# A 512-token transformer stream on one core: modulation sums placed earlier in the first mixer, the softmax scale folded into the keys, the last square root taken on ScalarE

## The chip, the core and the metric

The kernel runs on one core of a Trainium2 chip. The metric is the device time in microseconds from the start to the end of one execution. The five engines of the core (TensorE, VectorE, ScalarE, GpSimd and SyncE) each run their own list of instructions strictly in order; they meet only at semaphores. In the rows below TensorE is PE, VectorE is DVE, ScalarE is ACT, GpSimd is POOL and SyncE is SP; SPq is the queue in which SP issues its transfers.

## What is computed

One stream of 512 tokens by 1024 features passes through two blocks. The first has a gated linear attention mixer and a convolutional feed-forward part, each closed by a residual with a modulation that depends on the conditioning vector `c`; the second has a retention layer and a layer of latent attention (MLA). Cut to what the change touches:

```python
def post_norm_residual(x, cs, w_mod, b_mod, ln_gain, ln_bias, sublayer):
    # shift, scale and gate come from cs @ w_mod + b_mod: the "modulation"
    ...

def gla_mixer(h, w_in, w_a2, b_a, norm_g, w_o):        # 4 heads, chunks of 64
    q, k, v, r, a_lr = jnp.split(h @ w_in, [...], axis=-1)
    log_a = jax.nn.log_sigmoid((a_lr @ w_a2 + b_a).astype(jnp.float32)) / GLA_TAU
    bcum = jnp.cumsum(chunks(log_a, GLA_DK), axis=3)
    q_dec = qf * jnp.exp(bcum)
    k_inv = kf * jnp.exp(-bcum)
    k_dec = kf * jnp.exp(blast - bcum)
    ...                                                # att, state, o
    o = o * lax.rsqrt(jnp.mean(o * o, -1, keepdims=True) + LN_EPS) * norm_g
    return (o * jax.nn.silu(r)) @ w_o

def mla_attention(q_nope, q_rope, k_nope, k_rope, v):  # 8 heads, blocks of 128 queries
    scale = (MLA_NOPE + MLA_ROPE) ** -0.5              # 192 ** -0.5
    sc = jnp.einsum('bqhd,bkhd->bhqk', qn_i, k_nope) + jnp.einsum('bqhr,bkr->bhqk', qr_i, k_rope)
    sc = sc.astype(jnp.float32) * scale
    sc = jnp.where(mask[None, None], sc, -jnp.inf)
    p = jax.nn.softmax(sc, axis=-1).astype(v.dtype)
    ...

def mla_layer(x, ...):
    y = (jax.nn.silu(gate) * o) @ w_out
    return x + rmsnorm(y, g_post)                      # the last root: rsqrt(mean(y*y) + eps)
```

## The kernel before

Every large product is done in three passes (`mm3`, L154, L155, L156): each factor is held as a high part, rounded to TensorE's fp32r format, and a low part with the rest, and the passes are high by high, high by low, low by high. `split` (L108) makes the two parts: ACT casts the high part (L114), DVE subtracts it for the low part (L115); with a scale, ACT scales while it rounds and DVE does multiply and subtract in one instruction (L118).

Weights come in 512 KB pieces: SP issues the transfer into `raw` (L127), ACT and DVE split the piece into `wsp`, TensorE multiplies. Both names are rings of four buffers. The ring of `raw` is shared: the pieces of the modulation matrices (`rawm`) take buffers from it as well, so a piece that waits for DVE holds a buffer that the next weights would need. There are two kinds of those pieces. Sixteen pieces of `l_mod` are each multiplied with a row and summed along it by one DVE instruction (L423; eight chunks, two sums each, into `mc1`), and thirty-two instructions over pieces of `mod_w` add up the gates (`macc`, L367).

The mixer runs in this order on TensorE: values of heads 0 and 1 with q and k, the low-rank decay input (`gla_a`, L597), the gate projection r for heads 0 and 1 with the decay products (L625) in between, then for heads 0 and 1 the inner products and state updates (`gla_inner`), then the same outputs (`gla_outer`, `po`), the values of heads 2 and 3 (`gla_v`), the transposes of the finished half u (`gate_T`, L462, evicted by DVE as `uT` through L118), inner products of heads 2 and 3, the gate r of those heads (`gla_r`, evicted by ACT as u at L485), and their outputs. The decay of a pair of heads goes through a chain on ACT and DVE: exponential and logarithm, a scan (L641), exponentials (L644, L648, L649), products with q and k (L662, L664), and splits into `qd` and `ki`, which the inner products (`aux<-qd,ki`) read.

Where the `l_mod` and `mod_w` pieces stand among this is set by the tuple `PLACE`: entry i says how many chunks are loaded and summed at the call `place(i)`. Within the constraints that `self.after(engine)` and priorities give, the framework orders the instructions of each engine when the program is built; on the chip nothing is reordered.

The MLA layer takes for each of 8 heads and 4 query blocks the scores in PSUM (`sc`), a maximum over the row (L1285, `mx`), that maximum times -scale (L1287, `nm`), the exponential with scale and bias (L1290, ACT), a reciprocal and a product for the weights `p`, and transposes of `p` (L1305). The final layer's `post_rms` (L1036) takes a reciprocal root per query block from `rsqrt` (L230): an integer guess and three Newton steps, nine DVE instructions on one value a row, and then scales and adds the residual (L1056 for blocks 0 to 2, L1081 in two halves for block 3, the last work of the program).

## Time and profile of the kernel before

| what | us |
|---|---|
| median of 3 runs (1264.45 to 1265.42) | 1265.42 |
| the profiled execution's own time | 1263.45 |
| its span, first to last instruction | 1261.7 |
| TensorE busy | 1223.8 (97%) |
| TensorE's wait for the first weights | 12.5 |
| VectorE busy | 816.8 (65%) |
| ScalarE busy | 540.4 (43%) |
| HBM traffic over the span | 117 GB/s |

A line of the timeline gives start, duration, engine, line of the kernel, operation, output and inputs, the number of like instructions joined in it, and in square brackets how long the engine had been idle before and whose work ended that. The durations of TensorE's matmuls overlap each other: the distance of two starts is what one costs.

### The profile page before, as it was taken

What the parts mean: (1) busy time and instruction counts of PE and PEld (TensorE: products, weight loads), DVE (VectorE), ACT (ScalarE), POOL (GpSimd) and SP (SyncE); (2) the same over time, 40 slices, a digit from 0 to 9 for tenths busy, and PEclk for the clock granted to TensorE, in tenths of its full rate; (3) what the DMA queues carried; (4) which work ended last, traced back from release to release, by engine and by line L of the source; (5) the groups of instructions that cost most, each with busy time, mean ns of one, the idle gap of its engine ahead of it and who ended that gap; (6) DMA issues with size and microseconds to landing.
All of it is one profiled execution on the core that took longest, in us unless ns stands there. A gap on an engine that the chain in (4) does not pass through costs nothing.

```text
span 1261.7 us, 16038 instructions
## 1 busy us (share of the span) xinstructions
PE 1223.8 (97%) x5982; PEld 1022.9 (81%) x5982; DVE 816.8 (65%) x1828; ACT 540.4 (43%) x958; POOL 3.6 (0%) x15
## 2 busy tenths in 40 slices
PE   6999899999999999999999999999999999999997
PEld 4777677898888888888788888888888888888886
DVE  6689587788442354445885648556454689677755
ACT  3585244443332133342443333433434347577631
POOL 0000000000000000000000000000000000000000
PEclk9999899999999999999999999999999999999999
DMA  9556275237222333334153232323332333212221
GB/s 363 201 168 231 79 254 172 64 120 231 87 98 100 101 91 93 100 123 128 63 157 90 85 89 85 92 84 92 117 105 96 109 98 107 70 51 75 84 84 68
DMA packets 133043, 148.44 MB, mean 118 GB/s; under 512 B 9825, under 2 KB 92152, under 8 KB 132964
## 3 DMA queue, kind: packets, MB, share of 16 engines
q1 hardware_dynamic: 132964, 147.40, 36.7%
q8 instruction: 47, 0.77, 0.3%
q14 instruction: 32, 0.26, 0.1%
HBM read 141.09 MB, written 6.29 MB: 117 GB/s over the span
## 4 chain that ended last, share of the span: by engine, by line
PE 84%; DVE 7%; ACT 4%; DMA 2%; issue 2%; SPq 0%; DVEq 0%; ACTq 0%
PE acc L154 25%; PE acc L156 25%; PE acc L155 25%; PE po L154 1%; PE po L156 1%; PE po L155 1%; DVE wsp L115 1%; DMA raw<-in_gla_w_in 1%; PE aux L154 1%; PE aux L155 1%; ACT wsp L114 1%; PE aux L156 1%; DVE rawm L423 1%; PE aux L931 1%; PE aux L1283 1%
## 5 line engine op out<-in xcount | busy, mean ns | idle before, releaser
L115 DVE TENSOR_TENSOR wsp<-raw,wsp 128x1024 fp32r<-128x1024 f32 (+1 forms) x162 | 195.5, 1209 | 183.8 <-ACT wsp L114 183.4
L114 ACT CAST wsp<-raw 128x1024 fp32r<-128x1024 f32 (+1 forms) x162 | 167.7, 1038 | 279.4 <-PE acc L156 239.3
L154 PE MATMUL acc<-hT,wsp 128*128 128x512 f32 (+1 forms) x640 | 244.0, 381 | 0.5 <-DVE v L115 0.5
L156 PE MATMUL acc<-hT,wsp 128*128 128x512 f32 (+1 forms) x640 | 243.0, 380 | 0.0
L155 PE MATMUL acc<-hT,wsp 128*128 128x512 f32 (+1 forms) x640 | 242.7, 379 | 0.0
L154 PE MATMUL acc<-wsp,hT 128*128 128x512 f32 (+2 forms) x448 | 170.2, 388 | 12.6 <-ACT wsp L114 12.5
L155 PE MATMUL acc<-wsp,hT 128*128 128x512 f32 (+2 forms) x448 | 171.6, 383 | 1.8 <-DVE wsp L115 1.8
L156 PE MATMUL acc<-wsp,hT 128*128 128x512 f32 (+2 forms) x448 | 170.1, 382 | 0.0
L154 PEld LDWEIGHTS acc<-hT,wsp 128*128 128x128 f32 x640 | 120.7, 189 | 23.6 <-DVE v L115 1.4
L155 PEld LDWEIGHTS acc<-hT,wsp 128*128 128x128 f32 x640 | 120.5, 188 | 22.0 <-issue 0.2
L156 PEld LDWEIGHTS acc<-hT,wsp 128*128 128x128 f32 x640 | 120.5, 188 | 21.9
L154 PEld LDWEIGHTS acc<-wsp,hT 128*128 128x128 f32 x448 | 85.0, 190 | 28.4 <-ACT wsp L114 13.0
L155 PEld LDWEIGHTS acc<-wsp,hT 128*128 128x128 f32 x448 | 84.7, 189 | 16.6 <-DVE wsp L115 2.5
L156 PEld LDWEIGHTS acc<-wsp,hT 128*128 128x128 f32 x448 | 84.5, 189 | 15.2
L154 PE MATMUL acc<-wsp,uT 128*128 128x512 f32 (+1 forms) x192 | 75.5, 393 | 0.0
L156 PE MATMUL acc<-wsp,uT 128*128 128x512 f32 (+1 forms) x192 | 74.9, 390 | 0.0
L155 PE MATMUL acc<-wsp,uT 128*128 128x512 f32 (+1 forms) x192 | 74.8, 389 | 0.0
L154 PE MATMUL acc<-wsp,p 128*128 128x512 f32 x144 | 56.8, 395 | 0.0
L155 PE MATMUL acc<-wsp,p 128*128 128x512 f32 x144 | 56.8, 395 | 0.0
L156 PE MATMUL acc<-wsp,p 128*128 128x512 f32 x144 | 56.8, 395 | 0.0
L833 DVE SCALAR_TENSOR_TENSOR cv<-acc,cols,cv 128x511 f32<-128x511 f32 x22 | 16.5, 749 | 58.1 <-ACT cv L832 58.1
L832 ACT ACTIVATE cv<-acc,cols 128x512 f32<-128x512 f32 x22 | 17.2, 780 | 83.1 <-PE acc L156 83.1
(358 smaller groups left out, 2063.6 us busy)
## 6 DMA issues: line engine op xcount, KB each, us to landing
raw<-in_w_in_a SPq DMA_DIRECT2D x48, 512.0 KB
raw<-in_ffn_w_up SPq DMA_DIRECT2D x44, 512.0 KB
raw<-in_ffn_w_down SPq DMA_DIRECT2D x22, 512.0 KB
ms<-in_l_mod SPq DMA_DIRECT2D x16, 512.0 KB
raw<-in_gla_w_in SPq DMA_DIRECT2D x16, 512.0 KB
rawm<-in_l_mod SPq DMA_DIRECT2D x16, 512.0 KB
rawm<-in_mod_w SPq DMA_DIRECT2D x16, 512.0 KB
raw<-in_w_out_a SPq DMA_DIRECT2D x16, 512.0 KB
```

Of the source, the lines that this page charges most:

```text
L114: nc.scalar.copy(hi, src)
L115: nc.vector.tensor_sub(lo, src, self.f(hi))
L154: mm(out, l[0], r[0], start=first, stop=False)
L155: mm(out, l[0], r[1], start=False, stop=False)
L156: mm(out, l[1], r[0], start=False, stop=last)
L423: nc.vector.scalar_tensor_tensor(m, m, 1.0, self.csr, op0=OP.mult, op1=OP.mult, accum_out=mc1[:, c, j:j + 1])
L832: nc.scalar.activation(t, p, AF.Identity, scale=cw[2 * NT + j], bias=cb[j])
L833: nc.vector.scalar_tensor_tensor(t[:, 1:], p[:, :T - 1], cw[NT + j], t[:, 1:], op0=OP.mult, op1=OP.add)
L931: nc.tensor.transpose(pu[:, b * P:(b + 1) * P], u[:, b, i * P:(i + 1) * P], self.ident)
L1283: nc.tensor.matmul(sc[:, :n], qrT[i][:, s], kr[i][:, :n], start=False, stop=i == 1)
```

## The change

It has three independent parts.

First, the places of the modulation sums. `PLACE` goes from seven entries to five: one chunk now stands before `gla_a`, two after the projection r as before, five chunks (ten sums) inside `gla_v`, at the last of its four weight pieces, and the two `mod_w` chunks after `gla_r` as before. The three chunks after the values' evictions and the three in heads 0 and 1 are gone from there. With it, all four weight pieces of r are split before the decay chain is written down, and the evictions of r to u are issued after that chain.

Second, in the MLA layer the factor 192 ** -0.5 is applied when the keys are split, so the scores come out scaled; the maximum is taken with a negation by the same instruction and the separate product is dropped.

Third, the reciprocal root of the final `post_rms` becomes a square root on ACT, a reciprocal and one Newton step.

```diff
--- before.py
+++ after.py
@@ -23,6 +23,7 @@
 ALPHA = 2.0 ** 0.25
 LN_EPS = 1e-5
 RMS_EPS = 1e-6
+SM = 192.0 ** -0.5
 FF = 2816
 MASKED = -float(2.0 ** 100)
 
@@ -245,6 +246,17 @@
             nc.vector.scalar_tensor_tensor(y, t, 1.5, y, op0=OP.add, op1=OP.mult)
         return y
 
+    def rsqrt_short(self, v):
+
+        nc = self.nc
+        y, t, h = self.small(1, "rs_y"), self.small(1, "rs_t"), self.small(1, "rs_h")
+        nc.scalar.activation(t, v, AF.Sqrt)
+        nc.vector.tensor_scalar_mul(h, v, -0.5)
+        nc.vector.reciprocal(y, t)
+        nc.vector.scalar_tensor_tensor(t, y, y, h, op0=OP.mult, op1=OP.mult)
+        nc.vector.scalar_tensor_tensor(y, t, 1.5, y, op0=OP.add, op1=OP.mult)
+        return y
+
     def transpose_split(self, dst, src, b, split_copy=True):
 
         nc = self.nc
@@ -271,7 +283,7 @@
     RAW, WSP, ST, MS = 4, 4, 6, 4
     GATES = {0: 4, 1: 5, 2: 6, 3: 7}
     WOUT = {6: (0, 2), 7: (2, 4)}
-    PLACE = (0, 2, 0, 0, 3, 3, 2)
+    PLACE = (1, 2, 0, 5, 2)
 
     def run(self):
         tc, nc = self.tc, self.nc
@@ -405,13 +417,6 @@
                 order = list(range(8)) + [(0, 2048), (0, 2560)]
 
                 def place(where):
-                    if where > 2:
-
-                        with self.after(nc.vector):
-                            return place_now(where)
-                    place_now(where)
-
-                def place_now(where):
                     for _ in range(self.PLACE[where]):
                         c = order.pop(0)
                         if isinstance(c, tuple):
@@ -424,19 +429,25 @@
                                                            accum_out=mc1[:, c, j:j + 1])
 
                 u = [out.tile([P, NB, 512], F32, name="u0")]
+                place(0)
                 arow = self.gla_a(ph, xT)
                 self.vectors(ph)
 
                 accs = [self.acc() for _ in range(NB)]
                 wi = a["gla_w_in"][0]
                 self.proj_t(xT, self.wsubs(wi, 2048, 2560, 0, 2), 512, None, accs=accs)
+                rest = [(k + 2, t) for k, t in self.wsubs(wi, 2048, 2560, 2, 8)]
                 with self.after(nc.tensor):
                     logs = self.gla_decay(ph, out, arow)
                 with tc.high_priority():
                     decay = [self.gla_sums(ph, out, logs, h) for h in range(2)]
-                place(0)
-                self.proj_t(xT, ((k + 2, t) for k, t in self.wsubs(wi, 2048, 2560, 2, 8)), 512,
-                            lambda b, ps: nc.scalar.activation(u[0][:, b, :], ps, AF.Silu), accs=accs)
+                chain = next(i for i in reversed(nc.cur_bb.bb.instructions) if i.engine == nc.scalar.engine)
+
+                def ev(b, ps):
+                    with tc.issue_after(chain):
+                        nc.scalar.activation(u[0][:, b, :], ps, AF.Silu)
+
+                self.proj_t(xT, rest, 512, ev, accs=accs)
                 place(1)
                 tril = out.tile([P, P], F32, name="tril")
                 nc.sync.dma_start(tril, a["k_tril"])
@@ -469,21 +480,23 @@
                     i0 = self.gla_inner(ph, p0, vh(0), tril)
                 with self.after(nc.scalar), self.after(nc.vector):
                     decay += [self.gla_sums(ph, out, logs, h) for h in range(2, 4)]
-                    place(3)
                 raw += self.gla_qk(xT, (2,))
                 i1 = self.gla_inner(ph, p1, vh(1), tril)
                 raw += self.gla_qk(xT, (3,))
-                place(4)
                 outer(0, i0)
                 outer(1, i1)
                 p2, p3 = prep(2), prep(3)
-                v = self.gla_v(out, xT, 1)
-                place(5)
+
+                def between():
+                    with self.after(nc.vector):
+                        place(3)
+
+                v = self.gla_v(out, xT, 1, between)
                 uT = [gate_T(0)]
                 i2 = self.gla_inner(ph, p2, vh(2), tril)
                 i3 = self.gla_inner(ph, p3, vh(3), tril)
                 self.gla_r(xT, 1, lambda b, ps: nc.scalar.activation(u[1][:, b, :], ps, AF.Silu))
-                place(6)
+                place(4)
                 for b in range(NB):
                     self.res[b] = self.main.tile([P, D], F32, tag=f"res{b}", name=f"res{b}")
                     nc.sync.dma_start(self.res[b], a["x"][0, b * P:(b + 1) * P, :])
@@ -565,10 +578,15 @@
         self.setup_late(ph)
         return xT, v, raws
 
-    def gla_v(self, out, xT, pr):
+    def gla_v(self, out, xT, pr, between):
+        def subs():
+            for k, t in self.wsubs(self.a["gla_w_in"][0], 1024 + pr * 512, 1536 + pr * 512):
+                if k == 6:
+                    between()
+                yield k, t
+
         v = out.tile([P, 2, NB, 512], F32R, tag="v", name="v")
-        self.proj_t(xT, self.wsubs(self.a["gla_w_in"][0], 1024 + pr * 512, 1536 + pr * 512), 512,
-                    lambda b, p: self.split(v[:, 0, b, :], v[:, 1, b, :], p))
+        self.proj_t(xT, subs(), 512, lambda b, p: self.split(v[:, 0, b, :], v[:, 1, b, :], p))
         return v
 
     def gla_r(self, xT, pr, evict):
@@ -1052,7 +1070,7 @@
             ms = self.small(1, "ms")
             nc.vector.tensor_add(ms, ss[b][:, 0:1], ss[b][:, 1:2])
             nc.vector.tensor_scalar(ms, ms, 1.0 / D, RMS_EPS, op0=OP.mult, op1=OP.add)
-            rs = self.rsqrt(ms)
+            rs = self.rsqrt_short(ms) if first else self.rsqrt(ms)
             nc.vector.scalar_tensor_tensor(self.res[b], y[b], rs, self.res[b], op0=OP.mult, op1=OP.add)
             done(b, slice(0, D))
 
@@ -1075,7 +1093,7 @@
                 nc.vector.tensor_scalar(sm, sm, 1.0 / D, RMS_EPS, op0=OP.mult, op1=OP.add)
             else:
                 nc.vector.tensor_scalar(ms, ms, 1.0 / D, sm, op0=OP.mult, op1=OP.add)
-                rs = self.rsqrt(ms)
+                rs = self.rsqrt_short(ms) if first else self.rsqrt(ms)
                 for s in (slice(0, 512), slice(512, D)):
                     r = self.res[b][:, s]
                     nc.vector.scalar_tensor_tensor(r, y[b][:, s], rs, r, op0=OP.mult, op1=OP.add)
@@ -1166,8 +1184,8 @@
                 ps = self.aux()
                 for b in range(NB):
                     nc.tensor.transpose(ps[:64, b * P:(b + 1) * P], krr[:, b, :], self.ident)
-                self.split(kr[0][0:64], kr[1][0:64], ps[0:64, :])
-                nc.scalar.copy(kr[0][64:128], ps[0:64, :])
+                self.split(kr[0][0:64], kr[1][0:64], ps[0:64, :], scale=SM)
+                nc.scalar.activation(kr[0][64:128], ps[0:64, :], AF.Copy, scale=SM)
                 for i, ts in ((0, qrT), (1, [kr])):
                     m = ph.tile([68, T], F32, name=f"mask{i}")
                     nc.sync.dma_start(m[64:68, :], a["k_msk"][i])
@@ -1260,9 +1278,10 @@
         nc.sync.dma_start(wl[:, 3:5, :], a["w_uk_2"][:, h * P:(h + 1) * P].rearrange("(k p) n -> p k n", p=P))
         ws = self.main.tile([P, 2, 5, P], F32R, tag="wsp", name="ws", bufs=self.WSP)
         self.split(ws[:, 0], ws[:, 1], wl)
-        for dst, src, k0, nk in ((qn, cqP, 0, 3), (kn, ckP, 3, 2)):
+
+        for dst, src, k0, nk, scale in ((qn, cqP, 0, 3, None), (kn, ckP, 3, 2, SM)):
             self.proj_f(src, [[(0, [(ws[:, 0, k0 + k, :], ws[:, 1, k0 + k, :]) for k in range(nk)])]],
-                        lambda n, p: self.split(dst[:, 0], dst[:, 1], p), nk=nk)
+                        lambda n, p: self.split(dst[:, 0], dst[:, 1], p, scale=scale), nk=nk)
         ps = self.aux()
         for b in range(NB):
             nc.tensor.transpose(ps[:64, b * P:(b + 1) * P], qr[:, b, h, :], self.ident)
@@ -1272,7 +1291,6 @@
 
     def mla_softmax(self, ph, qn, kn, kr, qrT):
         nc = self.nc
-        sm = 192.0 ** -0.5
         pr = []
         for b in range(NB):
             n = (b + 1) * P
@@ -1281,13 +1299,11 @@
             self.mm3(sc[:, :n], [qn[:, i, s] for i in range(2)], [kn[:, i, :n] for i in range(2)], True, False)
             for i in range(2):
                 nc.tensor.matmul(sc[:, :n], qrT[i][:, s], kr[i][:, :n], start=False, stop=i == 1)
-            mx = self.small(1, "mx")
-            nc.vector.reduce_max(mx, sc[:, :n], axis=AX.X)
             nm = self.small(1, "nm")
-            nc.vector.tensor_scalar_mul(nm, mx, -sm)
+            nc.vector.reduce_max(nm, sc[:, :n], axis=AX.X, negate=True)
             p = ph.tile([P, n], F32, tag=f"p{b}", name="p", bufs=2)
             den = self.small(1, "den")
-            nc.scalar.activation(p, sc[:, :n], AF.Exp, scale=sm, bias=nm, accum_out=den)
+            nc.scalar.activation(p, sc[:, :n], AF.Exp, bias=nm, accum_out=den)
             rd = self.small(1, "rd")
             nc.vector.reciprocal(rd, den)
             nc.vector.tensor_scalar_mul(p, p, rd)
```

On DVE, this is where before has the values' evictions (`v`) and the transposed u (`uT`) of the second half of the mixer:

```order
L722 SCALAR_TENSOR_TENSOR u_465<-po,rs_y,u_465 128x256 x4
L115 TENSOR_TENSOR v<-acc,v 128x512 x4
L423 SCALAR_TENSOR_TENSOR rawm,mc_462<-rawm,csr 128x1024 x4
L118 SCALAR_TENSOR_TENSOR uT_73<-aux,cols_494,uT_73 128x512
L423 SCALAR_TENSOR_TENSOR rawm,mc_462<-rawm,csr 128x1024 x2
L118 SCALAR_TENSOR_TENSOR uT_73<-aux,cols_494,uT_73 128x512 x3
L115 TENSOR_TENSOR kt<-aux,kt 128x384
```

Six sums thus stand between the last v and the last `uT`. And this is DVE of the change at the same evictions; `u_465` is u of heads 0 and 1, finished by L740:

```order
L740 SCALAR_TENSOR_TENSOR u_465<-po,rs_y,u_465 128x256 x4
L116 TENSOR_TENSOR v<-acc,v 128x512
L116 TENSOR_TENSOR wsp<-raw,wsp 128x1024
L116 TENSOR_TENSOR v<-acc,v 128x512 x2
L379 SCALAR_TENSOR_TENSOR macc<-rawm,cs,macc 128x512
L116 TENSOR_TENSOR v<-acc,v 128x512
L119 SCALAR_TENSOR_TENSOR uT_73<-aux,cols_500,uT_73 128x512 x4
L116 TENSOR_TENSOR wsp<-raw,wsp 128x1024
```

The six sums at L423 between `v` and `uT` are gone; the ten sums of `gla_v`'s call stand ahead of these lines, among the roots of the outputs of heads 0 and 1, and one sum for the gate (`macc`) now stands between the third and the fourth eviction of v.

On SP, before issues around the second values in this order (the `raw` at its top are the weights of `gla_v`, the four after the six `rawm` those of `gla_r`):

```order
L127 DMA raw<-in_gla_w_in 128x2x512 x3
L489 DMA res_1586<-in_x 128x1024
L127 DMA raw<-in_gla_w_in 128x2x512
L422 DMA rawm<-in_l_mod 128x1024 x6
L127 DMA raw<-in_gla_w_in 128x2x512 x4
L489 DMA res_1588<-in_x 128x1024
L364 DMA rawm<-in_mod_w 128x2x512 x2
```

The weights of `gla_r` come behind six pieces of `l_mod` there. The change has this order:

```order
L128 DMA raw<-in_gla_w_in 128x2x512 x4
L427 DMA rawm<-in_l_mod 128x1024
L502 DMA res_1586<-in_x 128x1024
L427 DMA rawm<-in_l_mod 128x1024 x9
L128 DMA raw<-in_gla_w_in 128x2x512 x4
L376 DMA rawm<-in_mod_w 128x2x512 x3
L502 DMA res_1588<-in_x 128x1024
```

The weights of `gla_r` still come behind all `rawm` of `l_mod`, but these now start right behind the weights of `gla_v`, and the first three pieces of `mod_w` follow the weights of `gla_r` directly.

In the first half, on DVE, before has behind the values of heads 0 and 1 the split of `was` (weights of the decay input), one weight piece, and `wr`, the low part of the weights of the decay products (made from `wf`):

```order
L115 TENSOR_TENSOR was<-wa,was 128x8x16
L115 TENSOR_TENSOR v<-acc,v 128x512 x4
L115 TENSOR_TENSOR wsp<-raw,wsp 128x1024
L618 TENSOR_TENSOR wr<-wf,wr 32x512
L348 COPY cols_494<-aux 128x127
L348 COPY cols_508<-aux 128x24
L601 TENSOR_TENSOR a_488<-acc,a_488 32x512
```

There `wr` comes behind one weight piece. The change:

```order
L428 SCALAR_TENSOR_TENSOR rawm,mc_462<-rawm,csr 128x1024
L116 TENSOR_TENSOR v<-acc,v 128x512 x4
L428 SCALAR_TENSOR_TENSOR rawm,mc_462<-rawm,csr 128x1024
L116 TENSOR_TENSOR was<-wa,was 128x8x16
L360 COPY cols_500<-aux 128x127
L360 COPY cols_514<-aux 128x24
L116 TENSOR_TENSOR wsp<-raw,wsp 128x1024
L619 TENSOR_TENSOR a_494<-acc,a_494 32x512
L116 TENSOR_TENSOR wsp<-raw,wsp 128x1024 x3
L636 TENSOR_TENSOR wr<-wf,wr 32x512
```

Two sums of the first chunk now stand around the evictions of v, and `wr` comes behind three more weight pieces. On TensorE the four decay products (`aux<-a,wr`) go from behind 24 products of r to behind 38.

## Rows read from the trace of the kernel before

**Rows 1.** Windows: us, busy us of PE, PEld, DVE, ACT, POOL, clock, DMA, GB/s

```profile
122.00:147.90 25.90, 25.70 (x128) 21.34 (x128) 11.93 (x42) 6.78 (x21) 0.00 (x0) 1.00 0.12 41
146.00:161.40 15.40, 9.40 (x49) 8.19 (x48) 12.20 (x22) 7.01 (x11) 0.99 (x2) 0.67 0.65 237
250.00:1000.00 750.00, 749.92 (x3544) 624.56 (x3543) 435.16 (x804) 273.13 (x401) 0.00 (x0) 1.00 0.35 106
```

**Rows 2.** Timeline of PE, five waits: start, duration, [idle <-releaser]

```profile
82.25 0.50 PE L155 MATMUL acc<-wsp,hT 128*128 128x512 f32 x1 [1.80 <-DVE wsp L115]
...
152.80 0.48 PE L154 MATMUL aux<-qd,ki 128*128 128x128 f32 x1 [4.90 <-DVE uT L118]
...
156.62 0.90 PE L680 MATMUL aux<-ident,qk 128*128 128x128 f32 x3 [1.00 <-DVE uT L118]
...
165.02 0.36 PE L154 MATMUL aux<-v,kt 128*128 128x256 f32 x1 [1.00 <-DVE sf L696]
...
189.53 0.39 PE L154 MATMUL po<-v,at 128*128 128x256 f32 x1 [1.60 <-ACT scr L717]
```

**Rows 3.** Waits of PE, 85 to 122 us: total us, times, longest

```profile
PE aux L154 <- ACT kt L114: 2.1, 2, 1.1
PE aux L154 <- DVE af L685: 0.6, 1, 0.6
```

**Rows 4.** Timeline of DVE around the second values

```profile
142.73 0.69 DVE L115 TENSOR_TENSOR v<-acc,v 128x512 fp32r<-128x512 f32 x1 [9.99 <-ACT v L114]
...
147.42 1.22 DVE L423 SCALAR_TENSOR_TENSOR rawm<-rawm,csr 128x1024 f32<-128x1024 f32 x1
...
152.00 0.75 DVE L118 SCALAR_TENSOR_TENSOR uT<-aux,cols,uT 128x512 fp32r<-128x512 f32 x1
...
154.67 1.23 DVE L423 SCALAR_TENSOR_TENSOR rawm<-rawm,csr 128x1024 f32<-128x1024 f32 x1 [0.78 <-DMA rawm<-in_l_mod]
...
155.82 2.06 DVE L118 SCALAR_TENSOR_TENSOR uT<-aux,cols,uT 128x512 fp32r<-128x512 f32 x3
```

**Rows 5.** Timeline of PE, neighbouring starts at half and full clock

```profile
153.93 0.41 PE L156 MATMUL aux<-qd,ki 128*128 128x128 f32 x1
154.14 0.41 PE L154 MATMUL aux<-qd,ki 128*128 128x128 f32 x1
...
161.35 0.27 PE L154 MATMUL aux<-qd,ki 128*128 128x128 f32 x1
161.46 0.28 PE L155 MATMUL aux<-qd,ki 128*128 128x128 f32 x1
```

**Rows 6.** Timeline of SP's queue, the weights of gla_r

```profile
150.97 5.33 SPq L127 DMA_DIRECT2D raw<-in_gla_w_in  x4
```

**Rows 7.** Page, part 2: GB/s moved in 40 equal slices

```profile
GB/s 363 201 168 231 79 254 172 64 120 231 87 98 100 101 91 93 100 123 128 63 157 90 85 89 85 92 84 92 117 105 96 109 98 107 70 51 75 84 84 68
```

**Rows 8.** Timeline of PE, then DVE: decay products, a key split

```profile
67.75 1.10 PE L625 MATMUL aux<-a,wr 96*128 96x512 f32 x4
...
84.59 0.69 DVE L115 TENSOR_TENSOR ki<-qk,ki 128x512 fp32r<-128x512 f32 x1
```

**Rows 9.** Timeline of the tail, DVE and ACT

```profile
1248.17 0.60 ACT L1048 ACTIVATE z<-acc 128x512 f32<-128x512 f32 x1 [4.86 <-PE acc L156]
...
1254.97 0.15 DVE L236 TENSOR_SCALAR rs_i<-msl 128x1 int32<-128x1 int32 x1
...
1256.70 1.41 DVE L1081 SCALAR_TENSOR_TENSOR res<-y,rs_y,res 128x512 f32<-128x512 f32 x2
```

**Rows 10.** Line L644, small ACT operations: ns min/median/max, starts

```profile
L644 ACT ACTIVATE em<-cum x4: 195/208/209, 79.5 to 103.1; 128x4 f32<-128x4 f32 x4
L644 ACT ACT_TABLE_LOAD  x2: 1283/1283/1283, 78.2 to 97.8; - x2
```

**Rows 11.** Waits of PE, 1090 to 1214 us; then line L1287

```profile
PE aux L1305 <- DVE ou L1318: 1.1, 2, 0.7
...
L1287 DVE TENSOR_SCALAR nm<-mx x32: 134/145/154, 1099.5 to 1205.8; 128x1 f32<-128x1 f32 x32
```

## The prediction, made before the changed kernel was run

> **What bounds the kernel now.** I read the windows first. Over 750 us in the middle TensorE is busy for 749.92 [rows 1], so no edit there can gain anything, and none that stays hidden can lose. What can move lies before 250 us and at the end. So the second view is the list of TensorE's waits by time: after the start it waits at 82.25 (1.80), twice between 85 and 122 for `kt` (2.1 in all), then 4.90, 1.00 and 1.00 around 147.9 to 165, and 1.60 at 189.53 [rows 2, 3]. The largest is named after `uT`, so the third view is DVE's timeline there. DVE sits idle for 9.99 us up to 142.73; then come the low parts of v, and at 147.42 four sums of `l_mod`, one `uT` at 152.00, two more sums to 155.82, of which the second waits 0.78 for its transfer, and only then the other three `uT` [rows 4]. TensorE has been out of work since 147.9. The work that it waits for is 0.7 us long and stands behind sums that nobody needs before the residual at the mixer's end.
>
> The clock adds to it. From 146.0 to 161.4 its mean is 0.67 [rows 1]; the levels here are full and half, so half of full speed held for (1 - 0.67) x 2 x 15.4 = 10.2 us, and the wait of 4.90 is the only long idle time before it. Neighbouring 128-column products start 0.21 apart there and 0.11 apart at 161.35 [rows 5]. The half-speed stretch ends at about 160.6, so TensorE works in it from 152.80 for 7.8 us less some 1.1 idle, 6.7 us; at full speed that is about 3.5. I put the clock's loss at 3.0 to 3.2 and take 3.0. **This place costs 4.90 + 1.00 + 0.1 + 1.00 + 3.0 = 10.0 us.**
>
> The sums hold up more: the last of their pieces wait for buffers, and SP issues the weights of `gla_r` behind them, only from 150.97 [rows 6].
>
> **Part one, the sums.** *At 147.9.* In the change no sum stands between v and `uT`. The ten sums begin when `gla_v`'s weights are split, near 122. DVE has 25.90 - 11.93 = 14.0 us free from there to 147.9 [rows 1], and ten sums at some 1.15 from start to start (147.42, then four to 152.00 [rows 4]) are 11.5. Six of them stood in this stretch's tail, so the room is enough. Their transfers set the pace: DMA is busy for 0.12 of that stretch [rows 1], and the best slice of the page moved 363 GB/s [rows 7], so a piece of 0.524 MB takes 1.44 us, ten 14.4, and the last sum ends at 137 to 139.5. Then DVE owes the two outputs' u and two weight splits, which I follow to 145.7, and v and one gate sum to 149.9; the four `uT` take 149.9 to 152.5 instead of 152.0 to 157.9. What is late next? TensorE, some 0.7 later than now (below), ends the transposes at 148.6 and waits 1.35 for the first `uT`, which frees a PSUM buffer; then 0.8 for the masked product, 0.25, and 1.4 for the third head's `kt`: 3.8. None is as long as the 4.90, so I expect no fall of the clock. Gain 10.0 - 3.8 = **6.2**. Bounds: all ten (10.0), or the sums' transfers late enough to leave everything as it is (0).
>
> *At 189.53.* The wait is for ACT, whose square of the outputs stands behind a cast that waits for a weight. With the weights of `gla_r` some 13 us earlier (issued from 135 to 139.5 after the tenth sum, not from 150.97) the next weights come sooner too: 1.60 becomes 0.3, gain **1.3**, bounds 0 to 1.6.
>
> *In the first half.* Here something is paid. All four weight pieces of r are split before the decay chain, so the 1.80 at 82.25 goes, and with r done early the `kt` waits change place. But one chunk's sums now stand around the first v, the transfers of `wf` come in SP's queue behind a weight piece whose buffer the second of these sums frees (at 58.5 by my working), and `wr` comes behind three more splits. The decay products start behind 38 products of r, not 24: 14 x 0.23 = 3.2 later, with the delay before them 71.3 instead of 67.75 [rows 8]. The chain behind them is latency on ACT and DVE, so `ki` of the first head, 84.59 now [rows 8], slips by 3.5 as well. TensorE has nothing else left from about 85.5: it waits 2.25 for the first `qd` and `ki`, 0.8 for the next, 0.9 for a PSUM buffer and a weight split, 1.25 for `kt` and the mask of the next head, 5.2 in all. Gone are 1.80 [rows 2] + 2.1 + 0.6 (the mask's, `af`) [rows 3] = 4.5. Net **-0.7**. Bounds: nothing new (+4.5); or the chain lands two us later and the clock falls as it did at 147.9 (-0.7 - 2 - 3.0 = -5.7).
>
> **Part two, the softmax.** 32 products of 0.145 us go [rows 11], each between maximum and exponential, 4.6 us of DVE latency on 32 paths. TensorE's waits in that layer are short, the largest 1.1 in two [rows 11]; only a chain that ends such a wait pays. I take **0.4**, bounds 0 to 1.1. Folding the scale turns eight plain subtractions into scaled ones (0.75 against 0.69, as `uT` and v in [rows 4]): 0.06 each, beside a busy TensorE, nothing; if that cover is gone, 0.5.
>
> **Part three, the root.** Nine DVE instructions from 1254.97 to 1256.70, 1.73 us [rows 9], or 0.19 each, stand on the path that ends the program. Instead: a small ACT operation (0.21 [rows 10]) with two changes of engine, which I put at 0.1 each, a reciprocal and two Newton instructions, 0.19 to 0.25 each: 0.21 + 0.2 + 0.6 = 1.0. Gain **0.7**, bounds 0.4 and 0.9. The roots of the other three blocks are hidden beside TensorE. The table for the root is loaded once, before the first of the four roots, between two squares, where ACT is idle for 4.86 [rows 9]; a load takes 1.28 [rows 10], so it costs nothing.
>
> A load in the rows is 1.28 and no more [rows 10]. The Trainium skill ("ScalarE: Activation LUTs", What ACT_TABLE_LOAD costs) adds a drain and states about 2.66 us for each change to another set; even that would fit under the 4.86, and by it the sum would be the same as long as no second load is paid at the end. I find none: squares follow roots without one in the order of the instructions.
>
> **The sum.** 6.2 + 1.3 - 0.7 + 0.4 + 0.7 = **7.9 us**. From the profiled execution's own 1263.45 that is 1255.5; this execution lies 2.0 below the median of 1265.42, so against the median I say **1257.5**.
>
> **Rivals.** *The gain is given back at the same place* (A). `uT` waits for the low parts of v, and these for ten sums paced by transfers, two roots, u, and now a gate sum behind a piece of `mod_w` between the third and the fourth v. Were a piece to take 2.0 us instead of 1.44, the ten would end near 145, `uT` near 158, and the 6.2 would be gone; 7.9 - 6.2 = 1.7, so 1263.7. For it: sums do wait for transfers today (0.78 [rows 4]). Against it: the rings run freely there, and DMA is nearly empty.
>
> *The first half pays the clock* (B). TensorE then idles for some 4 us of the 6 after 85.5, and half speed follows as it did behind 147.9. That costs 3 to 5 us: 1260.5 to 1262.5. Against it: no single idle time is over 2.3 in my working.
>
> *Slower* (C). The place is the decay chain at 60 to 90 us. `wf` now waits in SP's queue behind the fourth weight piece, and this behind the first chunk's second sum on DVE. From `wf` on nothing hides a delay, since TensorE has run out of r by 85.5: each us more is one us lost, plus 3.0 once the clock falls. The change is slower when the chain is more than 4.9 us later than my working (4.9 + 3.0 = 7.9), and beyond measurement from 7.5 us: 1268. For it: the change moves `wf` behind DVE's work and moves nothing out of its way. Against it: the pieces of the first chunk are issued first of all, and I count them as landed before v ends.
>
> *The root gets no shorter* (D). The two changes of engine may cost 0.5 each, or the table be loaded at the last root: 0.7 becomes 0 or -0.6, 1258.2 to 1258.8.
>
> By the Trainium skill (the same page, Table sets: the hidden batching unit) each set has one costly function of its own, and cheap ones are in every set; were the square not in the root's set, each change back would be a load, and one would stand at the end: the second case of D. The order of the instructions shows one load in that stretch.
>
> **How the numbers follow.** Forecast 0.56, D 0.10, B 0.11, A 0.13, C 0.10. A measurement of this kernel can tell about 0.2% from no change, 2.5 us: faster is below 1262.9, slower above 1267.9. Forecast, D and nearly all of B are faster, with a little of A: 0.75; the rest of A and the milder part of C are the same: 0.16; slower 0.09. The range: low is the forecast with the first half paying nothing (4.5 + 0.7 better) held against the other terms' smaller ends, 1253; high takes in A, 1264.
>
> **What would show it.** In the changed kernel's trace: DVE without an idle stretch of 10 us before the second v and no sum between v and `uT`; `uT` done near 152.5; the clock at full through 147 to 165; the wait for `qd,ki` at 85 to 88 of about 2.3; no wait of 1.6 before `po`; one table load among the last squares, and 1.0 us from the last sum to the residual. The prediction is wrong if the clock falls in the first half, if `uT` ends after 156, or if the decay products start after 73.

## The result, and the profile after

The changed kernel takes 1253.38 us (median of 4 runs, 1252.62 to 1256.79), the kernel before 1265.42 beside it; the ratio is 0.9911 with a 95% interval of 0.9898 to 0.9925. That is 0.9% faster, inside the range on record and 4 us below the forecast of 1257.5. The profiled execution has a span of 1250.8 us against 1261.7. Its own time is 1252.62 us against 1263.45: the two profiled executions are 10.8 us apart, the medians 12.0, and the account below is of the profiled ones. The total lies in the range, and the place at 147.9 did what was foreseen; but one term of the sum was three times too small, and the largest single surprise, some 5 us, stood in no term at all.

The windows of the changed kernel (us; busy us of PE, PEld, DVE, ACT and POOL; clock, DMA share, GB/s) answer to [rows 1]:

```profile
80.00:90.00 10.00, 7.49 (x37) 5.91 (x35) 9.41 (x15) 9.32 (x15) 0.00 (x0) 1.00 0.59 164
90.00:95.00 5.00, 4.47 (x18) 3.63 (x18) 5.00 (x9) 4.99 (x9) 0.00 (x0) 0.66 0.68 203
...
122.00:147.90 25.90, 25.90 (x131) 21.59 (x130) 23.72 (x65) 10.42 (x26) 0.99 (x2) 1.00 0.76 250
146.00:161.40 15.40, 12.85 (x83) 10.59 (x82) 15.39 (x27) 8.79 (x17) 0.00 (x0) 1.00 0.67 215
```

From 146.0 to 161.4 the clock is now 1.00 (0.67 before) and TensorE is busy for 12.85 us (9.40 before). DVE, which had 14.0 us free between 122.0 and 147.9, has 2.2. But a short stretch at half speed has appeared behind 90 us: (1 - 0.66) x 2 x 5.0 = 3.4 us. That the clock falls in the first half is one of the prediction's own signs of being wrong.

TensorE's longest waits in the timeline (start, duration, [idle and who ended it]) answer to [rows 2, 3]:

```profile
88.52 0.33 PE L155 MATMUL aux<-qd,ki 128*128 128x128 f32 x1 [2.24 <-ACT ki L115]
89.61 0.33 PE L157 MATMUL aux<-qd,ki 128*128 128x128 f32 x1 [0.27 <-DVE ki L116]
...
91.47 0.79 PE L155 MATMUL acc<-hT,wsp 128*128 128x512 f32 x1 [0.53 <-ACT u L448]
...
183.64 0.38 PE L155 MATMUL po<-v,at 128*128 128x256 f32 x1 [1.23 <-ACT scr L735]
```

The waits view puts the others in one row each (total us, times, longest):

```profile
PE aux L155 <- ACT kt L115: 2.5, 2, 1.4
...
PE aux L155 <- DVE uT L119: 1.0, 1, 1.0
PE acc L156 <- DVE wsp L116: 0.8, 1, 0.8
```

The wait for `uT` is 1.0 instead of 4.90 + 1.00. And this is DVE around the second values, which answers to [rows 4]:

```profile
138.68 1.23 DVE L428 SCALAR_TENSOR_TENSOR rawm<-rawm,csr 128x1024 f32<-128x1024 f32 x1 [0.62 <-DMA rawm<-in_l_mod]
...
139.98 1.22 DVE L428 SCALAR_TENSOR_TENSOR rawm<-rawm,csr 128x1024 f32<-128x1024 f32 x1
...
147.07 0.69 DVE L116 TENSOR_TENSOR v<-acc,v 128x512 fp32r<-128x512 f32 x1
...
150.00 0.75 DVE L379 SCALAR_TENSOR_TENSOR macc<-rawm,cs,macc 128x512 f32<-128x512 f32 x1
...
151.26 2.72 DVE L119 SCALAR_TENSOR_TENSOR uT<-aux,cols,uT 128x512 fp32r<-128x512 f32 x4
```

The tenth sum ends at 141.2, no sum stands between v and `uT`, and the gate sum between the third and fourth v waits for nothing. `uT` is done at 154.0.

Where the time went is read best from how far TensorE is ahead or behind at the same product of the two programs (start in the change minus start before):

| at TensorE's product | before | change | difference |
|---|---|---|---|
| decay input (`acc<-hT,was`, first) | 58.38 | 58.36 | 0.0 |
| decay products (`aux<-a,wr`, first) | 67.75 | 72.01 | +4.3 |
| transposes of u (`aux<-ident,u`, first) | 146.00 | 148.44 | +2.4 |
| tail of the mixer (`acc<-wt,uT`, first) | 218.72 | 214.30 | -4.4 |
| second half of the feed-forward part (`acc<-wsp,p`, first) | 379.63 | 375.24 | -4.4 |
| the same, last | 588.61 | 581.74 | -6.9 |
| MLA layer (`acc<-wrs,cqT`, first) | 1081.24 | 1072.87 | -8.4 |
| last product | 1253.51 | 1243.71 | -9.8 |
| the execution's own time | 1263.45 | 1252.62 | -10.8 |

The first half costs 2.4, the second half of the mixer gives 6.8, and so far this is the argument on record. Then 4.0 us more are won between 375 and 1072, a stretch in which TensorE was busy nearly all the time in both kernels (0.6 us of waits, at its end) and in which the change edits nothing.

### The profile page after: what moved, and what is told of

Read it like the earlier page. It is cut to its first block, busy times and chain, and to the rows that moved or that the text cites. A ratio compares the mean times of both kernels' runs of the same rounds, so it can differ in the third digit from the quotient of the medians.

```text
span 1250.8 us, 16003 instructions
## 1 busy us (share of the span) xinstructions
PE 1217.9 (97%) x5982; PEld 1020.5 (82%) x5982; DVE 809.3 (65%) x1776; ACT 543.2 (43%) x963; POOL 3.6 (0%) x15
## 4 chain that ended last, share of the span: by engine, by line
PE 83%; DVE 8%; ACT 5%; issue 2%; DMA 2%; SPq 0%; DVEq 0%; ACTq 0%
PE acc L155 25%; PE acc L156 25%; PE acc L157 25%; PE po L155 1%; PE po L157 1%; PE po L156 1%; DVE wsp L116 1%; PE aux L157 1%; PE aux L155 1%; PE aux L156 1%; ACT wsp L115 1%; DVE rawm L428 1%; PE aux L949 1%; DVE macc L379 1%; DMA raw<-in_gla_w_o 1%
```

## The experiments

### What was won where nothing was edited

Between 375 and 582 no wait goes, because there was none. The products themselves are closer together. This is the same window of 50 us in the feed-forward part for the kernel before, products with `p` alone (us, busy us, count, clock, DMA share, GB/s):

```profile
385.00:435.00 50.00, 50.00 (x217) 1.00 0.30 93
```

and for the change:

```profile
385.00:435.00 50.00, 50.00 (x222) 1.00 0.33 102
```

TensorE did 222 products instead of 217 in it, at full clock both times: 0.2267 us from start to start instead of 0.2324. Over 432 such products that is 2.5 us, which is the step from -4.4 to -6.9. The change dropped one thing that every later part feels: the small tile `mx` of the softmax, four buffers of 32 bytes. All pools that are laid out after the small tiles lie 128 bytes lower in SBUF than before. In the two programs as they are built, `p` went from an address of 224 modulo 256 to one of 96, and the weights `wsp`, the other operand, are at 96 in both. In the kernel before, products of `wsp` with `hT`, which is at 96 as well, are not slow; these two starts there are ten products apart, 2.27 / 10 = 0.227:

```profile
55.66 0.39 PE L154 MATMUL acc<-hT,wsp 128*128 128x512 f32 x1
...
57.93 0.39 PE L155 MATMUL acc<-hT,wsp 128*128 128x512 f32 x1
```

So the theory was: a product is slower when its two operands do not lie at the same address modulo 256 bytes. The rival: the spacing belongs to the execution, not to the kernel.

**The change, moved back by 128 bytes.**

```diff
 def mla_softmax(self, ph, qn, kn, kr, qrT):
     nc = self.nc
+    if not hasattr(self, "spare"):
+        self.spare = self.small(1, "spare")
+        nc.gpsimd.memset(self.spare, 0.0)
```

> The changed kernel with one 128-byte tile added back to the pool of small tiles, in the place of the one (mx) that the change dropped; it is written once by GpSimd and never read, so every later pool lies 128 bytes higher, where it lay before the change. Address theory: the products of the feed-forward part's second half go back from 0.2267 to 0.2324 us apart (432 of them, 2.5 us), those of the retention and MLA outputs and of the MLA queries lose some 2.3 more, those of the mixer's output win 0.5: about 4.3 us slower than the change, 1257.7, ratio to before 0.994. Rival (the whole gain comes from waits and the clock, and the spacing is of the execution): no difference, 1253.4, ratio 0.990.

Measured: 1260.33 us, ratio 0.9955 (0.9940 to 0.9970). The same window has 217 products again:

```profile
385.00:435.00 50.00, 50.00 (x217) 1.00 0.30 93
```

Behind the mixer TensorE's lead over the kernel before changes by only 0.3 us, the size of the softmax's part, where the change wins 5.4. The rival is out. The loss is larger than foreseen, 0.44% or 5.6 us, and more time at half speed goes with it: its profiled execution has 10.2 us of it up to 120 us, the change's 3.4, and the granted clock of its four executions is 0.994 to 0.996 where the change has 0.995 to 0.998.

**The kernel before, moved by 128 bytes**, with the same three lines and nothing else.

> The kernel before with the same 128-byte tile added, so that every later pool lies 128 bytes higher; distances modulo 256 bytes are then those of the change, and nothing else differs. Address theory: 4.3 us faster than before, 1261.1, ratio 0.9966, with the spacing of acc<-wsp,p at 0.2267. Rival: no difference, ratio 1.000.

Measured: 1259.83 us, ratio 0.9952 (0.9937 to 0.9967): 6 us for a tile that nobody reads. Its window:

```profile
385.00:435.00 50.00, 50.00 (x222) 1.00 0.32 99
```

Its lead over the kernel before grows by 5.1 us from the tail of the mixer to the last product: 2.5 in the feed-forward part, 1.6 in the retention layer, 1.0 in the MLA layer. That is the size of the term that the prediction did not have.

**The spacing by itself.** The kernel's work was left out; groups of 48 products ran with the operands at set distances. A stationary tile has 1056 bytes, so each lies 32 bytes further modulo 256 than the one before.

```diff
+for k in range(8):
+    st[k] = pool.tile([P, 264], F32R, name=f"st{chr(97 + k)}")
...
+    for i in range(N):
+        h = i % 2
+        nc.tensor.matmul(acc[:, :n], s[:, h * P:h * P + P], m[:, off + h * 512:off + h * 512 + n],
+                         start=i == 0, stop=i == N - 1)
```

> The kernel's work is left out: groups of 48 products, moving operand of 512 columns always at the same address, stationary operands at addresses that differ by 0, 32, 64, 96, 128, 160, 192 and 224 bytes modulo 256 from it (sta to sth), then the moving operand 128 bytes further against the stationary at its own address modulo 256 (ste) and 128 off (sta), then 256 and 128 columns at difference 0 and 128. Address theory: the spacing is 0.2267 where the two addresses agree modulo 256 and about 0.232 where they differ by 128, for both moving operands, so it is the difference that counts and not the address; the other differences are open. Rival: 0.2267 in all groups.

The timeline of that kernel, from the second group on (start, duration, tiles, shape, count); the difference of two starts, divided by 48, is the spacing:

```profile
15.66 11.28 PE L37 MATMUL ac<-mv,sta 128*128 128x512 f32 x49
26.78 11.35 PE L37 MATMUL ac<-mv,stb 128*128 128x512 f32 x48
37.97 11.36 PE L37 MATMUL ac<-mv,stc 128*128 128x512 f32 x48
49.17 11.40 PE L37 MATMUL ac<-mv,std 128*128 128x512 f32 x48
60.41 11.32 PE L37 MATMUL ac<-mv,ste 128*128 128x512 f32 x48
71.56 11.37 PE L37 MATMUL ac<-mv,stf 128*128 128x512 f32 x48
82.77 11.16 PE L37 MATMUL ac<-mv,stg 128*128 128x512 f32 x48
93.76 11.36 PE L37 MATMUL ac<-mv,sth 128*128 128x512 f32 x48
104.95 11.35 PE L37 MATMUL ac<-mw,sta 128*128 128x512 f32 x48
116.14 11.09 PE L37 MATMUL ac<-mw,ste 128*128 128x512 f32 x48
127.07 5.92 PE L37 MATMUL ac<-mv,sta 128*128 128x256 f32 x48
132.83 5.85 PE L37 MATMUL ac<-mv,ste 128*128 128x256 f32 x48
138.52 5.47 PE L37 MATMUL ac<-mv,sta 128*128 128x128 f32 x48
143.82 5.52 PE L37 MATMUL ac<-mv,ste 128*128 128x128 f32 x48
```

With equal addresses (`sta`) the spacing is 11.12 / 49 = 0.2269. At 32, 64, 96, 160 and 224 bytes it is 0.2331 to 0.2342, at 128 0.2323, at 192 0.2290. For the second moving operand, 128 bytes further, it is 0.2331 against `sta`, which is 128 off now, and 0.2277 against `ste`, which agrees: it is the difference that counts. With 256 columns the spacing at 128 is 0.1185 against 0.1200, with 128 columns 0.1117 against 0.1105: 1% either way in one group each, so no loss is shown for them. The theory holds, and it is sharper than foreseen: each of the seven differences that were tried costs 1 to 3% on a product of 512 columns. Why the chip does this was not shown; the runs show only when.

**The parts apart.** Part one alone, with all its edits in the mixer (`place`, `rest`, `ev`, `between`), keeps the tile and so the old addresses.

```diff
-    PLACE = (0, 2, 0, 0, 3, 3, 2)
+    PLACE = (1, 2, 0, 5, 2)
```

> Part one of the change alone (the places of the modulation sums, r's weights split ahead, r's evictions behind the chain); softmax and root are those of before, and the dropped tile stays, so the addresses are those of before. Address theory: the mixer's own gain, about 4.9 us on TensorE, is all: 1260.5, ratio 0.996. Rival (all but root and softmax is the sums'): 1265.4 - 10.3 = 1255, ratio 0.992. Both: the wait for qd,ki at 85 to 89 of about 2.2 and a short stretch at half clock behind it.

Measured: 1260.87 us, ratio 0.9955 (0.9939 to 0.9972). From the decay input to the tail of the mixer TensorE wins 5.2 us on the kernel before, and from there to the last product nothing more (0.1 us of change). The rival's 1255 is out. Part one alone (0.45%) and the shift alone (0.48%) make up the 0.89% of the change within the intervals, which are about 0.15% either way; parts two and three, below, are 0.1%.

**Part two alone**, with the scale in the splits of the keys and a tile of the same size in the place of `mx`.

```diff
-    nc.vector.reduce_max(mx, sc[:, :n], axis=AX.X)
-    nc.vector.tensor_scalar_mul(nm, mx, -sm)
+    nc.vector.reduce_max(nm, sc[:, :n], axis=AX.X, negate=True)
-    nc.scalar.activation(p, sc[:, :n], AF.Exp, scale=sm, bias=nm, accum_out=den)
+    nc.scalar.activation(p, sc[:, :n], AF.Exp, bias=nm, accum_out=den)
```

> Part two alone on the kernel before: scale in the keys, negated maximum, 32 DVE products fewer; the tile that this drops is replaced by one of the same size, so no address moves. First theory (the gain forecast for this part, 0.4, is its own): TensorE's lag against the kernel before changes by -0.3 to -0.5 between 1080 us and its last product. Rival (what the change wins there comes from addresses): no change, under 0.1.

A single execution, 1264.48 us beside 1265.36. TensorE's lag goes from +1.36 at the MLA layer's first product (1082.60 against 1081.24) to +1.04 at the last product of all (1254.55 against 1253.51): 0.32 us. The theory holds, at the low end.

**Part three alone.**

```diff
-    rs = self.rsqrt(ms)
+    rs = self.rsqrt_short(ms) if first else self.rsqrt(ms)
```

> Part three alone on the kernel before: from the start of the last product to the start of the residual's last addition 2.35 us instead of 3.19, 0.8 less, nothing else different; one table load between two squares. Rival (two changes of engine cost 0.5 each): 0.2 less or nothing.

A single execution, 1263.15 us. The last product starts at 1253.92 and the last addition at 1256.26, so 2.34 us lie between them and 3.19 before: 0.85 won. The changed kernel has the same 2.35:

```profile
1243.71 0.28 PE L157 MATMUL aux<-wsp,uT 128*128 128x256 f32 x1
...
1245.18 0.20 ACT L253 ACTIVATE rs_t<-msl 128x1 f32<-128x1 f32 x1 [0.61 <-DVE msl L1095]
...
1246.06 1.41 DVE L1099 SCALAR_TENSOR_TENSOR res<-y,rs_y,res 128x512 f32<-128x512 f32 x2
```

Its one table load stands between two squares, before the first of the four roots:

```profile
1228.17 1.28 ACT L253 ACT_TABLE_LOAD   x1
```

### What the first half costs, and why

The change is 2.4 us late when the second values are done, and the forecast had 0.7. Two of its edits stand there: the first chunk's sums ahead of the decay input, and r's weights split ahead of the decay chain. Three kernels take them back, one by one and together. (The third edit there, r's evictions behind the chain, was taken back only together with the others.) after_no_first:

```diff
-    PLACE = (1, 2, 0, 5, 2)
+    PLACE = (0, 3, 0, 5, 2)
```

> The change with the first chunk's two sums moved from ahead of the decay input to the place behind r (entries 0 and 1 of the table of places 0 and 3 instead of 1 and 2); r's pieces are still all split ahead of the decay chain. The decay products then stand behind 28 products of r instead of 38 (24 before the change). First theory (the chain's delay is what the first half costs, and it comes from both edits): of the 3.1 us that the change is late at the first outputs about two thirds come back, the wait for qd,ki falls from 2.24 to under 1 and the clock stays full. Rival (splitting r ahead is the cause): the wait stays at about 2 and half clock follows.

A single execution, 1252.59 us. Counted from the decay input (executions are up to 2.7 us apart there, see the end) the decay products are 0.9 late instead of 4.3, the wait for `qd,ki` falls to 1.47, and at the tail of the mixer TensorE is 6.1 ahead of the kernel before, 1.7 more than the change; by its one time it can't be told from the change. But the clock did fall:

```profile
88.00:98.00 10.00, 9.25 (x36) 7.56 (x37) 9.21 (x15) 8.28 (x14) 0.00 (x0) 0.66 0.69 203
```

So the chunk's sums were the larger part of the delay, and neither theory is right about the clock. after_lazy_r:

```diff
-    rest = [(k + 2, t) for k, t in self.wsubs(wi, 2048, 2560, 2, 8)]
-    self.proj_t(xT, rest, 512, ev, accs=accs)
+    self.proj_t(xT, ((k + 2, t) for k, t in self.wsubs(wi, 2048, 2560, 2, 8)), 512, ev, accs=accs)
```

> The change with r's three later weight pieces loaded and split when their products are written, as before the change; the first chunk's two sums stay around the first values' evictions. The decay products stand behind 24 products of r. First theory (38 products instead of 24 are the delay): the decay products start near 68, no wait of 2 for qd,ki, no half clock there, the 1.8 us wait for a low part of r's weights is back: about 2 us earlier at the first outputs than the change. Rival (the sums around v, and wf behind them in SP's queue): the decay products stay near 72 and the wait stays.

A single execution, 1259.35 us, 6 us worse than the change (4.8 by TensorE's last product, counted from the decay input); both theories missed. The decay products are 1.1 late only, as the first theory had it, but then TensorE starves:

```profile
81.28 2.08 PE L155 MATMUL acc<-wsp,hT 128*128 128x512 f32 x4 [3.91 <-ACT wsp L115]
85.30 0.79 PE L156 MATMUL acc<-wsp,hT 128*128 128x512 f32 x1 [1.94 <-DVE wsp L116]
```

because on ACT the casts of r's last two pieces now stand behind the exponentials and logarithms of the chain:

```profile
78.30 2.00 ACT L648 ACTIVATE em<-em 128x1024 f32<-128x1024 f32 x2
80.20 1.98 ACT L115 CAST wsp<-raw 128x1024 fp32r<-128x1024 f32 x2
```

The clock is 0.61 from 78 to 91. Splitting r ahead is thus no cost of the change but what saves it from this, as long as the first chunk's sums stand there. Why the casts come out so late in that order was not followed up; that the chunk's two pieces hold buffers of the same ring is a guess. after_half, with the lines of before from `u` to the projection r:

```diff
-    PLACE = (1, 2, 0, 5, 2)
+    PLACE = (0, 3, 0, 5, 2)
...
-                place(0)
...
-                rest = [(k + 2, t) for k, t in self.wsubs(wi, 2048, 2560, 2, 8)]
...
-                self.proj_t(xT, rest, 512, ev, accs=accs)
+                self.proj_t(xT, ((k + 2, t) for k, t in self.wsubs(wi, 2048, 2560, 2, 8)), 512,
+                            lambda b, ps: nc.scalar.activation(u[0][:, b, :], ps, AF.Silu), accs=accs)
```

> The change with the whole first half as before (no chunk ahead of the decay input, r's pieces and evictions as before, three chunks behind r instead of two); the ten sums inside the second values' loop, softmax, root and addresses are the change's. First theory (the first half costs the change 3 us of what the rest gains): 2 to 3 us faster than the change, ratio to before 0.989 against 0.991. Rival (another wait takes the place, the 1.8 and 1.06 of before come back and more): as the change or slower.

Measured: 1252.44 us, ratio 0.9898 (0.9881 to 0.9914). TensorE is 7.8 us ahead at the tail of the mixer, counted from the decay input, against 4.4 for the change; the 1.8 at r's weights is back, the wait for `qd,ki` is gone. The time says 1.6 us, the trace 3.4; the intervals of the two ratios overlap, so that it beats the change rests on the trace. At the tail of the mixer it is also 1.7 us ahead of after_no_first, which differs from it only in r's weights split ahead and r's evictions behind the chain: without the chunk these gain nothing. The clock fell in it twice, for 3.4 us each: behind the 1.8, and at 153.6, where it stays full in the change:

```profile
146.00:161.00 15.00, 13.19 (x81) 11.47 (x80) 14.99 (x27) 8.38 (x16) 0.00 (x0) 0.89 0.68 206
```

### Every pair of operands aligned

In the change, `wt` of the mixer's and of the feed-forward tail, and the mixer's `uT`, still disagree with the other operand. Three tiles made larger cure that, on top of after_half:

```diff
-mb1 = self.mod.tile([P, 8, 2], F32, name="mb1")
+mb1 = self.mod.tile([P, 48], F32, name="mb1")[:, :16].rearrange("p (k j) -> p k j", j=2)
-sums = self.tail.tile([P, NB, 2], F32, name="sums")
+sums = self.tail.tile([P, 64 if affine else 32], F32, name="sums")
+sums = sums[:, :2 * NB].rearrange("p (b n) -> p b n", n=2)
```

> The kernel after_half with three tiles made larger so that the mixer's outputs (uT) and the two tail pools' weights (wt) also lie at the same address modulo 256 bytes as the other operand of their products. Address theory: acc<-wsp,uT of the mixer from 0.2325 to 0.2267 (96 products, 0.56 us), acc<-wt,uT of the mixer and acc<-wt,p from 0.2335 to 0.2267 (192 products, 1.3 us): 1.9 us faster than after_half, ratio about 0.9875. Rival (only a difference of 128 bytes costs): 0.6 us, as these pools lie 32 or 96 bytes off.

Measured: 1251.35 us, ratio 0.9887 (0.9872 to 0.9902), the fastest here. The mean of the products with `wt,p` shows it; lines, engine, operation, tiles, shape, count, busy us, mean ns, first of this kernel:

```profile
L156 PE MATMUL acc<-wt,p 128*128 128x512 f32 x32 | 12.5, 389 | 0.0
```

then of the change:

```profile
L156 PE MATMUL acc<-wt,p 128*128 128x512 f32 x32 | 12.6, 395 | 0.0
```

From start to start that is 0.2269 instead of 0.2334, although `wt` had been only 32 bytes off, as the address map has it and the rival has not. Against after_half the time gives 1.1 us, within the interval; 1.9 had been foreseen. From the tail of the mixer to the last product the trace gives 0.6 us where the tails should give 1.3: with the products closer together TensorE waits longer for `res` between 215 and 250 (1.0 us in all, 0.6 in after_half), and for 0.16 us more at 592.

**The kernel before with all four tiles**, nothing of the change.

> The kernel before with the four tiles made larger (the 128 bytes of before_shifted, and those of half_aligned), so that both operands of every product with 512 columns that had a slow spacing agree modulo 256 bytes; not an instruction of the work differs. Address theory: 5.1 us behind the mixer as in before_shifted, 0.5 in the mixer that before_shifted lost comes back, 1.3 in the tails: 6.4 us faster than before, 1259.0, ratio 0.995. Rival (the shift worked through something else than the difference of the two addresses): as before_shifted or slower.

Measured: 1259.39 us, ratio 0.9952 (0.9934 to 0.9970). By the trace it wins 5.5 us from the decay input to the last product, where before_shifted wins 4.0 and 6.4 was foreseen; by the time the two can't be told apart. From the tail of the mixer on it wins 5.5 against 5.1, with the same waits for `res`: here too the tails give less than half of their 1.3.

## Why the prediction was right, and where it was not

The time lies in the range, and the largest part of the argument, the place at 147.9, came as told. By one of its own signs the prediction is wrong all the same: the clock fell in the first half. The other two did not come (`uT` at 154.0, not after 156; the decay products at 72.01, not after 73).

**The place at 147.9: right.** The mechanism is as told: sums out of the way, `uT` at once, no fall of the clock. Ten sums were to end at 137 to 139.5 and ended at 141.2. They started at 125.04 instead of near 122, as the first half had made the work ahead of them late. Their transfers set the pace only at the end: the trace has waits of 0.69, 0.25 and 0.62 for them, 1.6 of the 16.1 us; the rest is the sums (1.15 each) and the small operations of the roots between them. DVE then works without a pause, so `uT` ended 1.5 later than told for the same reason. The new waits were 1.01, 0.48 and 1.06, so 2.55 where 3.8 was put: the sum for this place would have been 7.4, not 6.2. That the clock stays full there holds for this execution; in after_half, with the same edits at that place, it fell for 3.4 us.

**The wait at 189.53: too much hoped for.** 1.60 became 1.23, not 0.3. ACT still waits for transfers, now of the next weights, before it evicts u, and the table load for that stands behind them too:

```profile
177.49 1.05 ACT L115 CAST wsp<-raw 128x1024 fp32r<-128x1024 f32 x1 [1.68 <-DMA raw<-in_gla_w_o]
...
179.87 1.28 ACT L498 ACT_TABLE_LOAD   x1
181.16 2.06 ACT L498 ACTIVATE u<-acc 128x512 f32<-128x512 f32 x4
183.09 0.41 ACT L735 ACTIVATE scr<-po 128x256 f32<-128x256 f32 x1
```

The step took the casts to be the only work ahead of `scr`; four evictions and a load were. The size of this wait is not settled by the edits: with the same instructions in the mixer it is 1.07 us in after_shifted_back and under 0.1 in only_sums.

**The first half: the term that was mis-sized.** -0.7 was put and -2.4 measured. Two things are missing in that step. First, on DVE the copies of `cols` come ahead of r's first weight piece in the change (the order has it, the working passed it by); they wait for TensorE's transposes, and TensorE then waits 0.80 for that piece:

```profile
62.38 0.38 DVE L360 COPY cols<-aux 128x127 f32<-128x127 f32 x2 [4.17 <-PE aux L359]
62.68 1.21 DVE L116 TENSOR_TENSOR wsp<-raw,wsp 128x1024 fp32r<-128x1024 f32 x1
```

With it the decay products start at 72.01, not 71.3. Second, the clock: the wait for `qd,ki` was forecast at 2.25 and is 2.24, and "no single idle time is over 2.3" was the reason against half speed; but half speed came, for 3.4 us. By size it is the clock that was missed: from the decay input to the transposes of u TensorE waits for 6.0 us in the change and 5.0 before, a net loss of 1.0 where 0.7 was put, and the other 1.4 of the 2.4 is about what 3.4 us at half speed, less a wait of 0.53 in them, can cost. That is rival B in a mild form, and it was given 0.11. The experiments say more: the stretch at half speed came in every kernel with that wait, and behind the 1.47 of after_no_first too. Behind the wait of 1.8 for r's weights it came in before_shifted, after_half and half_aligned and not in the kernel before, only_softmax, only_root and before_aligned. Shorter waits were followed by it too: 1.37 at 114.0 in after_shifted_back and 1.16 at 151.9 in after_half, where the change has 1.41 at 110.9 and 1.01 at 152.1 and stays at full speed. Its length differs as well (3.4 and 6.8 us for the same first half). So the wait's length alone does not tell it, and what does is open.

**The addresses: a term that was not there.** The prediction looked at the order of instructions and at their durations, and took every product of 512 columns to cost the same before and after. The sentence "no edit there can gain anything" on the stretch in which TensorE is always busy is wrong: it holds for waits, not for the products' own spacing. The spacing was 0.2324 with `p` and 0.227 with `hT` already in the trace of before. 5.0 of the 10.8 us come from there, less 0.5 that the mixer's `uT` lost by moving out of line (96 products).

**The softmax** was put at 0.4 and is 0.32 by itself; **the root** at 0.7 and is 0.84. The one table load took 1.28 between two squares, with 3 us of idle ACT behind it, and so cost nothing. The Trainium skill ("ScalarE: Activation LUTs", What ACT_TABLE_LOAD costs) adds a drain to the load at each change of set, about 2.66 us together; this trace does not show it, as the root starts at 1229.46, 1.29 after the load's start, and by either price the load is hidden.

With these sizes the sum is 7.4 + 0.4 - 2.4 + 5.0 - 0.5 + 0.3 + 0.8 = 11.0, against 10.8. It closes better than its parts: the second half of the mixer gave 6.8 where 7.4 + 0.4 - 0.5 = 7.3 are put. The terms that the forecast had come to 6.5, short of its 7.9; the addresses, which it did not have, add 4.5. That the time still lies in the range, by 0.4 us, is luck: its lower end was reached by another way, a first half that pays nothing, and that did not happen.

## What to carry to other kernels

Before a product's spacing is taken as given, compare it across the program: the same shape at two spacings in one trace is a gain that needs no edit of the work. Dropping or adding a small tile moves every pool behind it, so a timing change in parts that were not touched is first to be looked for in the addresses, and an experiment that removes a tile should put one of the same size in its place. Work that nobody waits for belongs where its engine idles, but the buffers and the queue it passes through on the way belong to the price.

## What the runs showed of the hardware that was not expected

- A product of 512 columns in fp32r, with new weights for each, starts 0.2267 us after the one before when the moving and the stationary operand lie at the same address modulo 256 bytes, and 0.2323 to 0.2342 after it at six other differences, 0.2290 at 192. With 256 and 128 columns a difference of 128 shows no clear loss (1% less and 1% more, one group each).
- TensorE's granted clock has stretches at half speed (0.5 of full) whose length is not the same from execution to execution: 3.4 and 6.8 us for the same first half of the mixer, and behind the wait of 4.9 at 147.9 10.2 us in three kernels and 6.8 in two others (only_root, before_aligned) with the same work there.
- The first product starts between 12.5 and 14.8 us after the span's start, by when the first weights land; the difference is in the times, and comparisons of two single executions have to take it out.
